# Moving the split activations to the other end of SBUF

## The chip, the cores and the metric

The kernel runs on one core of a Trainium2 chip. The metric is the device time of one execution in microseconds; smaller is better. The time before is the median of three runs. The time of the one execution that was profiled stands in the table below, since all rows come from it.

## The reference, cut to what matters

Two transformer blocks, one after the other, on 256 tokens of width 1024, all in float32. The first block projects its normed input (`w_in`), runs two attentions with eight heads each, gates and merges them, and ends in an MLP of width 4096. The second block projects again (`w_in_2`), mixes by spatial gating and a dilated attention, and ends in PEER, which is most of the time:

```
q = (xb @ w_query).reshape(PEER_TOKEN_BLOCK, PEER_HEADS, 2, D_KEY // 2)
...
g = jax.nn.softmax(sc, axis=-1)
u = expert_u[e]
act = jax.nn.gelu(jnp.einsum('td,thkd->thk', xb, u).astype(jnp.float32))
return jnp.einsum('thk,thkd->td', (g * act).astype(xb.dtype), expert_v[e])
```

Here 16 experts of 16,384 are chosen for each of the 256 tokens and 8 heads. The kernel doesn't gather them: it computes `x @ expert_u.T` for all experts, multiplies by a dense table of weights, and multiplies the result by `expert_v`. Both tables have 64 MB.

## The kernel before, in words

**Split products.** Each float32 operand of a large product is split in two parts, a rounded one and the rest: `wh` and `wl` for weights, `hh` and `hl` for activations. `mm3` (L164) makes one product of three matmuls: high by high, high by low, low by high, with `hh` and `wh` the high parts. TensorE takes two operands from SBUF: the weights that it loads (the stationary operand) and the ones that it streams through.

**Two kinds of stage.** In a *station* stage (`stations`, L288: w_gate, w_up, w_query, expert_u) the stored weights are stationary and the activations are streamed, 256 columns a matmul (two blocks of 128 tokens). A unit has two tiles of 1024 columns, 24 matmuls each, so 48 matmuls. In the other stages (`projecting` L251, `rows_product` L272, `down` L613, `v_units` L1042) the activations are stationary and the stored weights are streamed, mostly 512 columns a matmul.

**Weights.** `weights` (L107) takes tiles in turn from a cycle of pools. SP's queue loads `raw` (512 KB each), ACT copies it to `wh` (L115), and VectorE or GpSimd subtracts to give `wl` (L121). The pool `ring` has four buffers each of `raw`, `wh` and `wl`. From w_branch to w_query the cycle alternates `wkx, ring` (L564), and for the MLP two places of the right-hand pool `wk` are added behind those eight (L600). In the expert stages there is only `ring`.

**Activations.** `parts` (L210) allocates `hh` and `hl`, 8192 bytes of each partition for either. Where it is called without a pool they come from `hp`, which has one buffer of each and is used for the first projections and w_gate (L422), w_out (L568), w_in_2 (L628), and the PEER input that w_query and expert_u use (L721); at the end two tiles of it hold the residual (L1062). The MLP's own `hh` and `hl` (L591) come from the right-hand pool `wk`, and w_branch streams `oah`, `oal`, `obh`, `obl` from a right-hand pool too.

**SBUF.** A pool lies on the left or the right and is a stack: a later pool lies further in, and one that is closed gives its bytes back. Bytes per partition, as the kernel before has them:

| tiles | pool, side | from | to |
|---|---|---|---|
| raw, four buffers | ring, left | 19,744 | 36,128 |
| wh, four buffers | ring, left | 36,128 | 52,512 |
| wl, four buffers | ring, left | 52,512 | 68,896 |
| small things | small, left | 68,896 | 70,176 |
| hh, hl | hp, left | 70,176 | 86,560 |
| further left pools from here on | xp, wk1, wkx, pk, ab, pv | 86,560 | |
| wh, four buffers from w_branch to w_query | wkx, left | 123,008 | 139,392 |
| ah, two buffers in expert_v | pv, left | 152,096 | 156,192 |
| hh, hl of the MLP | wkm (`wk`), right | 161,760 | 178,144 |
| oah, the first of w_branch's four | wk1b, right | 192,480 | 196,576 |
| wh, two buffers in the MLP | wkm (`wk`), right | 206,816 | 215,008 |
| right end of the pools | | | 229,344 |

**Order of the work in PEER.** w_query has four station units and expert_u 64. TensorE's instructions are kept in program order (`in_line`, L137). During the first 32 units of expert_u (L982) VectorE also does the selection of experts (`route`). During the last 32 (L1032) each step of 12 matmuls is followed by the products that make the dense table of weights (`weighted`, L992): for two tokens VectorE makes two one-hot tiles each, `m1` and `m2` (L1019, L1020, six buffers each), and TensorE multiplies those of two earlier tokens; VectorE then multiplies the results into `acts` (L1008, L1011). After that expert_v runs with 64 units of 24 matmuls, with `ah` and `al` stationary.

Of the kernel before, what the change touches and what calls it, by code (L numbers as in the profile page):

```python
# [75 lines left out]
def block_kernel(ctx: ExitStack, tc: tile.TileContext, a, out, dbg=None):  # L76
# [3 lines left out]
    const = ctx.enter_context(tc.tile_pool(name="const", bufs=1))  # L80
    ring = ctx.enter_context(tc.tile_pool(name="ring", bufs=1))
    small = ctx.enter_context(tc.tile_pool(name="small", bufs=4))
    hp = ctx.enter_context(tc.tile_pool(name="hp", bufs=1))
    ps = ctx.enter_context(tc.tile_pool(name="ps", bufs=1, space=PSUM))
    dram = ctx.enter_context(tc.tile_pool(name="dram", bufs=1, space=DRAM))
    xres = dram.tile([P, TB, D], F32, name="xres")
# [1079 lines left out]
```

## Time and profile before

| | |
|---|---|
| median of 3 runs | 1369.34 us (1367.41 to 1370.09) |
| profiled execution | 1366.17 us |
| its span, first to last instruction | 1364.4 us |
| PE busy | 1320.8 us, 97% |
| PEld (weight loads, beside PE) busy | 1178.1 us, 86% |
| DVE (VectorE) busy | 982.0 us, 72% |
| ACT busy | 667.1 us, 49% |
| POOL (GpSimd) busy | 198.0 us, 15% |
| mean granted TensorE clock | 0.993 |

PE is TensorE. The busy time of an engine is the union of its instructions' durations. Matmuls are pipelined: a matmul's row lasts about 0.28 us for 256 columns while the next one starts some 0.12 us after it, so a busy TensorE says little, and the distance of starts says more. The chain of waits is followed back from the last instruction, at each step to what released it or to the instruction before it on its engine. A row of windows has the window, its length, then the busy time of PE, PEld, DVE, ACT and POOL, each with its count of instructions, and then the granted clock, the DMA share and GB/s.

### The profile page before, as it was taken

What the parts mean: (1) busy time and instruction counts of PE and PEld (TensorE: products, weight loads), DVE (VectorE), ACT (ScalarE), POOL (GpSimd) and SP (SyncE); (2) the same over time, 40 slices, a digit from 0 to 9 for tenths busy, and PEclk for the clock granted to TensorE, in tenths of its full rate; (3) what the DMA queues carried; (4) which work ended last, traced back from release to release, by engine and by line L of the source; (5) the groups of instructions that cost most, each with busy time, mean ns of one, the idle gap of its engine ahead of it and who ended that gap; (6) DMA issues with size and microseconds to landing.
All of it is one profiled execution on the core that took longest, in us unless ns stands there. A gap on an engine that the chain in (4) does not pass through costs nothing.

```text
span 1364.4 us, 22115 instructions
## 1 busy us (share of the span) xinstructions
PE 1320.8 (97%) x8324; PEld 1178.1 (86%) x8324; DVE 982.0 (72%) x2255; ACT 667.1 (49%) x1018; POOL 198.0 (15%) x103
## 2 busy tenths in 40 slices
PE   6999898999998999999999999999999999999997
PEld 5788896799986677999999999999978888888886
DVE  6666678555568795799994799999975555555555
ACT  5576545444444655355454444443435444544443
POOL 2221224322235336200000000000000000000001
PEclk9999999999999999999999999999999999999999
DMA  7453464666645425356666544444456666666662
GB/s 282 159 182 113 145 214 142 209 188 187 191 136 187 127 76 190 103 177 191 177 190 181 166 140 140 140 140 140 138 182 192 197 189 197 192 194 189 197 194 86
DMA packets 64187, 230.61 MB, mean 169 GB/s; under 512 B 7280, under 2 KB 7696, under 8 KB 63952
## 3 DMA queue, kind: packets, MB, share of 16 engines
q1 hardware_dynamic: 61632, 221.03, 52.5%
q0 software_dynamic: 1728, 6.07, 1.2%
q10 hardware_dynamic: 720, 2.10, 0.4%
q8 instruction: 65, 1.06, 0.3%
q14 instruction: 42, 0.34, 0.1%
HBM read 227.07 MB, written 2.10 MB: 168 GB/s over the span
## 4 chain that ended last, share of the span: by engine, by line
PE 90%; DVE 6%; ACT 2%; DMA 1%; issue 1%; SPq 0%; ACTq 0%; DVEq 0%
PE acc L135 52%; PE mid L135 35%; DVE wl L121 2%; PE tps L145 2%; DMA x<-in_x_dram 1%; ACT wh L115 1%; PE tps L135 1%; DVE x L244 0%; DVE ny L234 0%; DVE at_s L340 0%; ACT ny L206 0%; DVE rope_t L311 0%; DMA raw<-in_w_branch_dram 0%; DVE hl L174 0%; DVE at_s L332 0%
## 5 line engine op out<-in xcount | busy, mean ns | idle before, releaser
L115 ACT ACTIVATE wh<-raw 128x1024 fp32r<-128x1024 f32 (+2 forms) x422 | 439.2, 1047 | 421.7 <-PE mid L135 238.4
L121 DVE TENSOR_TENSOR wl<-raw,wh 128x1024 fp32r<-128x1024 f32 (+1 forms) x350 | 447.7, 1281 | 216.0 <-ACT wh L115 215.4
L135 PE MATMUL mid<-hh,wh 128*128 128x256 f32 x1280 | 372.1, 291 | 0.0
L135 PE MATMUL mid<-hh,wl 128*128 128x256 f32 x1280 | 361.2, 282 | 0.0
L135 PE MATMUL mid<-hl,wh 128*128 128x256 f32 x1280 | 361.0, 282 | 0.0
L135 PEld LDWEIGHTS mid<-hl,wh 128*128 128x128 f32 x1280 | 244.5, 191 | 0.4
L135 PEld LDWEIGHTS mid<-hh,wh 128*128 128x128 f32 x1280 | 244.1, 191 | 0.4
L135 PEld LDWEIGHTS mid<-hh,wl 128*128 128x128 f32 x1280 | 243.9, 191 | 0.0
L121 POOL TENSOR_TENSOR wl<-raw,wh 128x1024 fp32r<-128x1024 f32 (+3 forms) x72 | 176.3, 2458 | 340.4 <-ACT wh L115 297.3
L135 PE MATMUL acc<-wh,ah 128*128 128x512 f32 x512 | 200.0, 391 | 2.9 <-ACT ah L173 2.9
L135 PE MATMUL acc<-wl,ah 128*128 128x512 f32 x512 | 199.9, 390 | 0.0
L135 PE MATMUL acc<-wh,al 128*128 128x512 f32 x512 | 199.8, 390 | 0.0
L135 PE MATMUL acc<-wh,hh 128*128 128x512 f32 (+2 forms) x288 | 116.1, 403 | 1.1 <-ACT hh L173 0.9
L135 PEld LDWEIGHTS acc<-wh,ah 128*128 128x128 f32 x512 | 96.4, 188 | 23.2 <-ACT ah L173 3.1
L135 PEld LDWEIGHTS acc<-wh,al 128*128 128x128 f32 x512 | 96.6, 189 | 20.6 <-DVE al L174 0.4
L135 PEld LDWEIGHTS acc<-wl,ah 128*128 128x128 f32 x512 | 96.6, 189 | 19.9
L135 PE MATMUL acc<-wl,hh 128*128 128x512 f32 (+2 forms) x288 | 113.0, 392 | 0.6 <-POOL wl L121 0.3
L135 PE MATMUL acc<-wh,hl 128*128 128x512 f32 (+2 forms) x288 | 112.6, 391 | 0.4 <-DVE hl L174 0.2
L1020 DVE TENSOR_SCALAR m<-tok,key,gwt 128x128 f32<-128x128 f32 x256 | 89.2, 349 | 0.0
L173 ACT ACTIVATE ah<-acts 128x512 fp32r<-128x512 f32 x64 | 40.3, 632 | 91.8 <-PE acc L135 89.2
L174 DVE TENSOR_TENSOR al<-acts,ah 128x512 fp32r<-128x512 f32 x64 | 44.3, 693 | 52.8 <-ACT ah L173 52.8
L1019 DVE TENSOR_SCALAR m<-tok,key 128x128 f32<-128x128 f32 x256 | 73.7, 289 | 6.5 <-PE acc L135 5.6
(259 smaller groups left out, 1703.2 us busy)
## 6 DMA issues: line engine op xcount, KB each, us to landing
raw<-in_expert_u_dram SPq DMA_DIRECT2D x128, 512.0 KB, 3.7
raw<-in_expert_v_dram SPq DMA_DIRECT2D x128, 512.0 KB, 4.5
raw<-in_w_down_dram SPq DMA_DIRECT2D x32, 512.0 KB, 4.4
raw<-in_w_up_dram SPq DMA_DIRECT2D x24, 512.0 KB, 4.7
raw<-in_w_in_dram SPq DMA_DIRECT2D x20, 512.0 KB, 4.7
raw<-in_w_gate_dram SPq DMA_DIRECT2D x16, 512.0 KB, 4.0
raw<-in_w_out_dram SPq DMA_DIRECT2D x16, 512.0 KB, 4.7
raw<-in_w_in_n_dram SPq DMA_DIRECT2D x12, 512.0 KB, 4.6
```

Of the source, the lines that this page charges most:

```text
L115: i = act.activation(h[:, :n], raw[:, :n], AF.Copy)
L121: last_split[0] = eng.tensor_tensor(l[:, :n], raw[:, :n], h[:, :n].bitcast(F32), op=OP.subtract)
L135: in_line(pe.matmul(p, x, y, start=start, stop=stop))
L145: in_line(pe.transpose(out, src, ident))
L173: turned_[0] = act.activation(h, p, AF.Copy)
L174: vec.tensor_tensor(l, p, h.bitcast(F32), op=OP.subtract)
L1019: vec.tensor_scalar(m2, i128, key2[:, t:t + 1], None, op0=OP.is_equal)
L1020: vec.tensor_scalar(m1, i128, key1[:, t:t + 1], gwt[:, t:t + 1], op0=OP.is_equal, op1=OP.mult)
```

## The change

The pool `hp` is opened on the right side. It stays the first pool that is opened there, and it is open until the end.

```
-    hp = ctx.enter_context(tc.tile_pool(name="hp", bufs=1))
+    hp = ctx.enter_context(tc.tile_pool(name="hp", bufs=1, side="right"))
```

## Rows read from the trace of the kernel before

**Rows 1.** Page, chain that ended last, by line: shares of the span.

```profile
PE acc L135 52%; PE mid L135 35%; DVE wl L121 2%; PE tps L145 2%; DMA x<-in_x_dram 1%; ACT wh L115 1%; PE tps L135 1%; DVE x L244 0%; DVE ny L234 0%; DVE at_s L340 0%; ACT ny L206 0%; DVE rope_t L311 0%; DMA raw<-in_w_branch_dram 0%; DVE hl L174 0%; DVE at_s L332 0%
```

**Rows 2.** Chain of waits in order of time: start us, duration us, what, count.

```profile
302.60 5.57 PE acc L135 x24
308.17 5.76 PE mid L135 x48
...
540.48 5.58 PE acc L135 x24
...
581.77 97.91 PE mid L135 x816
...
1005.16 347.64 PE acc L135 x1524
```

**Rows 3.** TensorE's timeline, w_up: start us, duration us, instruction.

```profile
285.69 0.28 PE L135 MATMUL mid<-hh,wh 128*128 128x256 f32 x1
...
288.56 0.28 PE L135 MATMUL mid<-hh,wh 128*128 128x256 f32 x1
...
291.28 0.40 PE L135 MATMUL acc<-wh,mfh 128*128 128x512 f32 x1
```

**Rows 4.** TensorE's timeline, w_branch (12 matmuls) and w_up (24), weights from ring.

```profile
179.20 0.28 PE L135 MATMUL acc<-oah,wh 128*128 128x256 f32 x1
...
180.61 0.28 PE L135 MATMUL acc<-obh,wh 128*128 128x256 f32 x1
...
266.15 0.28 PE L135 MATMUL mid<-hh,wh 128*128 128x256 f32 x1
...
268.98 0.39 PE L135 MATMUL acc<-wh,mfh 128*128 128x512 f32 x1
```

**Rows 5.** Windows in expert_u: busy us of each engine, with counts.

```profile
600.00:650.00 50.00, 50.00 (x419) 50.00 (x418) 50.00 (x134) 25.20 (x30) 0.00 (x0) 1.00 0.63 191
...
740.00:780.00 40.00, 40.00 (x339) 40.00 (x338) 23.64 (x53) 18.71 (x27) 0.00 (x0) 1.00 0.58 170
780.00:820.00 40.00, 40.00 (x343) 40.00 (x342) 37.58 (x121) 17.72 (x32) 0.00 (x0) 1.00 0.45 137
820.00:860.00 40.00, 40.00 (x343) 40.00 (x342) 38.53 (x121) 18.40 (x33) 0.00 (x0) 1.00 0.48 145
860.00:900.00 40.00, 40.00 (x342) 40.00 (x341) 39.08 (x126) 17.29 (x32) 0.00 (x0) 1.00 0.47 139
900.00:940.00 40.00, 40.00 (x343) 40.00 (x342) 39.66 (x121) 14.90 (x30) 0.00 (x0) 1.00 0.44 139
940.00:980.00 40.00, 40.00 (x343) 40.00 (x342) 40.00 (x124) 16.64 (x34) 0.00 (x0) 1.00 0.46 138
```

**Rows 6.** Timeline of ACT, VectorE and TensorE: one tile of expert_u's first half.

```profile
636.40 1.06 ACT L115 ACTIVATE wh<-raw 128x1024 fp32r<-128x1024 f32 x1 [1.34 <-PE mid L135]
...
639.50 1.23 DVE L121 TENSOR_TENSOR wl<-raw,wh 128x1024 fp32r<-128x1024 f32 x1
...
644.96 0.28 PE L135 MATMUL mid<-hh,wh 128*128 128x256 f32 x1
```

**Rows 7.** Chain of waits, last steps of expert_u.

```profile
996.97 1.43 PE mid L135 x12
...
998.85 1.43 PE mid L135 x12
1000.28 0.91 PE acc L135 x8
1001.19 0.29 DVE m L1019
```

**Rows 8.** Chain of waits, first attention with w_gate, and its end.

```profile
90.41 3.07 PE acc L135 x24
...
119.05 2.88 PE acc L135 x24
...
155.13 3.71 DMA raw<-in_w_branch_dram
```

## The prediction

> **What bounds the kernel now.** I read the chain of waits first, by line and then in order of time. By line it is TensorE's matmuls nearly everywhere [rows 1], so a change that TensorE does not feel is worth nothing, and one that it feels must be followed to the next engine. In order of time the chain shows long runs of matmuls without a gap: 816 in 97.91 us in the first half of expert_u, 1524 in 347.64 us in expert_v [rows 2]. A row's own duration is of no use here, because matmuls overlap; what counts is the pitch, from one start to the next. It is 97.91 / 816 = 120.0 ns for a matmul of 256 columns in expert_u. Then I read TensorE's timeline for the same matmul in other stages, and here the change has its place: the pitch is not the same everywhere. In w_up, which streams its own hh and hl from the right-hand pool, 24 matmuls with weights from the ring take 291.28 - 288.56 = 2.72 us, 113.3 each; the 24 before them, with weights from wkx, 288.56 - 285.69 = 2.87 us, 119.6 each [rows 3]. With weights from the right-hand pool (the last two places of the cycle) 48 take 5.76 us, 120.0 each [rows 2]. Shape, operands, PSUM tile and loop are the same in these three; only the places in SBUF differ. Two more stretches with weights from the ring give a third value: 24 in w_up take 268.98 - 266.15 = 2.83 us, 117.9 each, and 12 in w_branch, which streams oah and obh from the right, 180.61 - 179.20 = 1.41 us, 117.5 each [rows 4]. I looked at all ring tiles: of ten in w_up nine settle at 113.3 (two of them after a few slower ones) and one at 117.9; of eight in w_branch all go at 117.8. Within a tile the pitch keeps its value.
>
> **Where the change puts things.** No instruction, loop or DMA is added, removed or moved, so no queue is passed by anything. hp holds 8192 + 8192 bytes of each partition for the whole kernel, opened before every pool that follows and never closed. It goes from 70,176 to the right end, 229,344 - 16,384 = 212,960. const, ring and small lie before it and stay; every other pool, left or right, moves down by 16,384. So which tiles lie over which is the same as before, and with it every wait that comes of reused space. What differs is the distance between the tiles that move and the ring that does not. The rows can be ordered in two ways. By ends: streamed tile and weights at one end, 120.0 (expert_u, w_up's right-hand tiles); at opposite ends, 113.3 or 117.8. By the remainder of their distance in units of 128 bytes (it is the same for all tiles of a pair of pools, since buffers lie 4096 apart and each k steps 512 on both sides): 70,176 - 36,128 (expert_u) and 161,760 - 206,816 (w_up, right) leave 0 and go at 120.0; 161,760 - 36,128 (w_up, ring) and 192,480 - 36,128 (w_branch, ring) leave 64 and go at 113.3 or 117.8; 161,760 - 123,008 (w_up, wkx) leaves 96 and goes at 119.6. After the change 212,960 - 36,128 = 176,832 leaves 64, at opposite ends: by either order it falls among the rows with 113.3 or 117.8. No row shows this very place, so the bounds are 113.3 and 120.0, and I take 113.3 where a stream runs long, the nearer of the two lower values in loop and PSUM tile, although w_branch lies nearer to the new place.
>
> **The terms.** (1) expert_u's first 32 units, without expert products between: 32 x 48 x (120.0 - 113.3) = 10.2 us. VectorE must keep up. It is busy 50.00 of 50 us in 600 to 650 [rows 5], so there it can't go faster, and TensorE at 5.76 - 5.44 = 0.32 us less a unit eats up its lead. The lead is read from one tile: ACT writes its wh at 636.40, as soon as TensorE has left that buffer; VectorE's split, 1.23 us long, starts at 639.50 and TensorE takes the tile at 644.96, 4.2 us after the split [rows 6]. Some 12 units to here cost 3.9 us, just inside it; in 740 to 780 VectorE is busy 23.64 of 40 and the lead is won back. I take 0.2 us for the pinch: 10.0. If the lead fails earlier, I lose up to 2.
>
> (2) The second 32 units, with two expert products' worth of VectorE work behind every 12 matmuls. A step, 1.43 us of 12 matmuls of 256 columns and then the products, is 998.85 - 996.97 = 1.88 us [rows 7]; TensorE would get it down by 12 x 6.67 = 0.08 us, about 10 us over 125 steps. But VectorE has almost none to give: idle 2.42, 1.47, 0.92, 0.34 and 0.00 us in the 40 us stretches from 780 to 980 [rows 5], and after TensorE's last matmul here, 1000.28 + 0.91, VectorE still works alone from 1001.19 until expert_v starts at 1005.16 [rows 2, 7]. With TensorE at 1.80 of 1.88 a stretch of 40 us would take 38.3; VectorE needs 37.58 in the first, leaving 0.74 us of idle, and is the bound from the second on. So what goes is 2.42 + 1.47 + 0.92 + 0.34 - 0.74 = 4.4 us, and what is late next is VectorE: TensorE waits for the one-hot tiles, and its own gain of 10 shrinks to 4.4. Bounds 3 and 5.2.
>
> (3) w_gate, streamed from hp into the first attention: 24 matmuls take 3.07 us early and 2.88 later [rows 8], 128 and 120 each, broken up by other work. At 113.3, 384 matmuls would give 2.5 us; broken streams need not settle at the low value, and the stage ends on other things, last the landing of w_branch's first weights, 3.71 us [rows 8], whose buffer comes free earlier if TensorE is earlier. I take half, 1.2. (4) w_query: half its eight tiles have ring weights, 96 x 6.7 = 0.6 us less; the wkx half goes from remainder 32 to 96, whose row has 119.6, so at best nothing: I take 0.4 together.
>
> (5) The projections, with hp's tiles as weights and the ring streamed, 512 columns: 24 take 5.58 us now, 232.5 each; in w_down, whose weights lie at the right, 24 take 5.57 [rows 2]. So nothing, with 1.5 us either way. (6) expert_v: ah and al go down with the other left pools; ah at 152,096 - 36,128 leaves remainder 0 before and, 16,384 lower, after. I take its 347.64 / 1524 = 228.1 ns as it is.
>
> Sum: 10.0 + 4.4 + 1.2 + 0.4 = 16.0 us off the profiled execution's 1366.17 (span 1364.4), so 1350.2. The median of the runs is 1369.34, 3.2 us above that execution; what I predict is compared with such a median, so 1369.34 - 16.0 = 1353.3.
>
> A rule of the Trainium skill speaks against all this. SBUF — State Buffer, section "Who interferes with whom", gives TensorE two independent read ports, one for the streamed operand and one for the weight load, and says "PE and ACT never wait on anyone". By it the place of hp could not matter and the sum would be 0, which is rival (b). The trace disagrees: 113.3, 117.9 and 120.0 ns in one stage with only places differing [rows 2 to 4].
>
> **The rivals.** (a) The stream settles at 117.8, as in w_branch. Then term 1 is 1536 x 2.2 = 3.4 us, term 2 is what VectorE allows at 39.4 us for 40: 0.6 + 0.6 + 0.6 + 0.3 = 2.0 (its idle of 2.42, 1.47 and 0.92 each less by 0.6), terms 3 and 4 together 0.6: 6.0 us, 1363.3. For it: all of w_branch, and the one tile in w_up. Against it: nine tiles of ten in the stage that is most like expert_u.
>
> (b) The pitch stays at 120.0 in expert_u, because what the rows in w_up show comes of something else there, such as its alternation with w_down: no change, 1369.3. Against it: the right-hand tiles in the same alternation go at 120.0.
>
> (c) Slower: the order by remainder is wrong, expert_u stays at 120, and expert_v pays, since ah and al come 16,384 bytes nearer to the ring. The price is from w_down's mixed pitch, 5.57 / 24 = 232.1 against 228.1, 1536 x 4.0 = 6.1 us: 1375.4. It decides as soon as expert_v's pitch rises by more than expert_u's falls, matmul for matmul at about 1 to 1. Against it: ah, like hp now, keeps its remainder.
>
> **How the numbers follow.** My forecast has 0.55, (a) 0.25, (b) 0.13, (c) 0.07. About 0.2% of the time, 2.7 us, is what can be told from no change. The forecast and (a) are both faster by more: 0.80; (b) is the same, 0.13; (c) slower, 0.07. The forecast's own range goes from 1349 (w_gate whole, VectorE's idle all gone, projections 1.5 better) to 1358 (term 2 at 3, term 1 less by 2, projections 1.5 worse). With (a) and what its terms can miss the range is 1348.5 to 1366, leaving out (b) and (c).
>
> **What would show it.** In the changed profile: 24 ring matmuls of expert_u's first half 2.72 us apart, the run that is 97.91 us long for 816 now at 113.3 each; the second half's steps at 1.80 us at first and then stretched by waits for the one-hot tiles, with VectorE at 40.00 of 40 from early on; expert_v at 228 and the projections at 232 as before. A pitch of 117.8 is rival (a), 120.0 is (b). I am wrong in term 2 if the step reaches 1.80 us to the end, and in the whole if the pitch in expert_u falls but the stage doesn't get shorter.

## The result and the profile after

The changed kernel takes 1357.02 us (median of 4 runs, 1355.48 to 1358.35), the kernel before 1368.38 (4 runs of the same batch): ratio 0.9916, 95% interval 0.9897 to 0.9935. It is faster by 11.4 us where 16.0 were forecast; its median lies 3.7 us above the 1353.3 that was predicted, and inside the range of 1348.5 to 1366. A second batch of the unaltered changed kernel (below) gave 1353.69 against 1369.2, faster by 15.5. The profiled execution is one of 1355.48 us, its span 1353.7 (before: 1366.17 and 1364.4).

The chain by line, from the page after, answers to [rows 1]: TensorE still holds most of it, VectorE's split at L121 a little more than before.

```profile
PE acc L135 52%; PE mid L135 29%; DVE wl L121 3%; PE tps L145 2%; DMA x<-in_x_dram 1%; ACT wh L115 1%; DVE eq L896 1%; DVE ef L898 1%; PE tps L135 1%; DVE at_s L340 1%; DVE eq L893 1%; DVE x L244 0%; ACT ny L206 0%; DVE rope_t L311 0%; DVE ny L234 0%
```

The chain in order of time, after (start us, duration us, what, count), answers to [rows 2, 7, 8]:

```profile
90.89 2.94 PE acc L135 x24
...
118.95 2.75 PE acc L135 x24
...
303.56 5.57 PE acc L135 x24
309.12 5.76 PE mid L135 x48
...
542.68 5.58 PE acc L135 x24
...
583.35 40.83 PE mid L135 x360
...
687.93 54.46 PE mid L135 x478
...
984.91 1.38 PE mid L135 x12
986.29 0.44 PE acc L135 x4
986.73 1.42 PE mid L135 x12
...
994.54 347.55 PE acc L135 x1524
```

In expert_u 360 matmuls take 40.83 us, 113.4 ns each, and 478 take 54.46, 113.9; 816 took 120.0 each in [rows 2]. w_down (5.57), w_up's right-hand tiles (5.76), the projections (5.58) and expert_v (347.55) stand where they stood. In the second half of expert_u 12 matmuls take 1.38 and 1.42 us by turns, where [rows 7] have 1.43.

Windows in expert_u, after (busy us of PE, PEld, DVE, ACT, POOL with counts, granted clock, DMA share, GB/s), answer to [rows 5]:

```profile
600.00:650.00 50.00, 50.00 (x444) 50.00 (x443) 50.00 (x146) 27.03 (x32) 0.00 (x0) 1.00 0.61 189
650.00:700.00 50.00, 49.37 (x436) 49.17 (x435) 49.86 (x122) 26.58 (x34) 0.00 (x0) 1.00 0.63 194
740.00:780.00 40.00, 40.00 (x352) 40.00 (x351) 28.62 (x75) 19.33 (x30) 0.00 (x0) 1.00 0.56 171
780.00:820.00 40.00, 40.00 (x349) 40.00 (x348) 38.47 (x125) 18.74 (x33) 0.00 (x0) 1.00 0.48 141
820.00:860.00 40.00, 40.00 (x350) 40.00 (x349) 39.23 (x126) 17.98 (x33) 0.00 (x0) 1.00 0.47 142
...
940.00:980.00 40.00, 40.00 (x349) 40.00 (x349) 40.00 (x124) 15.91 (x32) 0.00 (x0) 1.00 0.46 135
```

TensorE gets 444 matmuls into 600 to 650 us where it had 419, and 349 or 350 into each stretch from 780 on that is shown, where it had 342 or 343.

Where the time went, by stage (us from the stage's first matmul to the next stage's, read from TensorE's timeline; w_up ends with its last matmul, and the rest of w_down counts with the way to w_query; expert_v goes to its last matmul; "again" is the second profile of the changed kernel, from the experiments):

| stage | before | after | again |
|---|---|---|---|
| start to w_gate | 87.56 | 88.06 | 87.53 |
| w_gate, first attention | 74.43 | 73.17 | 73.59 |
| w_branch to w_up | 101.30 | 103.02 | 100.84 |
| w_up, with w_down between | 117.38 | 117.38 | 117.38 |
| rest of w_down, to w_query | 166.48 | 167.73 | 166.47 |
| w_query | 27.74 | 27.41 | 27.41 |
| expert_u, first half | 185.91 | 176.72 | 176.68 |
| expert_u, second half | 239.20 | 234.40 | 234.39 |
| gap ahead of expert_v | 5.16 | 6.68 | 6.63 |
| expert_v | 349.95 | 349.87 | 350.13 |

The stages with a term lose 1.26 + 0.33 + 9.19 + 4.80 - 1.52 = 14.1 us. Three stages that the change does not touch take 0.50 + 1.72 + 1.25 = 3.5 us longer in the first profile of the changed kernel, and not in the second.

### The profile page after: what moved, and what is told of

It reads as the page before. It is cut to its first block, busy times and chain, and to the rows that moved or that the text cites. A ratio compares the mean times of both kernels' runs of the same rounds, so it can differ in the third digit from the quotient of the medians.

```text
span 1353.7 us, 22115 instructions
## 1 busy us (share of the span) xinstructions
PE 1308.4 (97%) x8324; PEld 1165.2 (86%) x8324; DVE 979.7 (72%) x2255; ACT 666.4 (49%) x1018; POOL 197.4 (15%) x103
## 4 chain that ended last, share of the span: by engine, by line
PE 84%; DVE 10%; issue 2%; ACT 2%; DMA 1%; SPq 0%; POOL 0%; ACTq 0%; DVEq 0%
PE acc L135 52%; PE mid L135 29%; DVE wl L121 3%; PE tps L145 2%; DMA x<-in_x_dram 1%; ACT wh L115 1%; DVE eq L896 1%; DVE ef L898 1%; PE tps L135 1%; DVE at_s L340 1%; DVE eq L893 1%; DVE x L244 0%; ACT ny L206 0%; DVE rope_t L311 0%; DVE ny L234 0%
## 5 line engine op out<-in xcount | busy, mean ns | idle before, releaser
L121 DVE TENSOR_TENSOR wl<-raw,wh 128x1024 fp32r<-128x1024 f32 (+1 forms) x350 | 449.2, 1286 | 208.9 <-ACT wh L115 208.5
L135 PE MATMUL mid<-hh,wh 128*128 128x256 f32 x1280 | 367.2, 287 | 0.0
L135 PE MATMUL mid<-hh,wl 128*128 128x256 f32 x1280 | 355.8, 278 | 0.6 <-DVE wl L121 0.6
L135 PE MATMUL mid<-hl,wh 128*128 128x256 f32 x1280 | 355.9, 278 | 0.0
L135 PEld LDWEIGHTS mid<-hl,wh 128*128 128x128 f32 x1280 | 241.9, 189 | 0.4
L135 PEld LDWEIGHTS mid<-hh,wh 128*128 128x128 f32 x1280 | 241.0, 188 | 0.4
L135 PEld LDWEIGHTS mid<-hh,wl 128*128 128x128 f32 x1280 | 240.5, 188 | 0.8 <-DVE wl L121 0.8
L121 POOL TENSOR_TENSOR wl<-raw,wh 128x1024 fp32r<-128x1024 f32 (+3 forms) x72 | 175.0, 2441 | 343.9 <-ACT wh L115 301.1
L135 PE MATMUL acc<-wh,ah 128*128 128x512 f32 x512 | 200.0, 391 | 2.9 <-ACT ah L173 2.9
L135 PE MATMUL acc<-wl,ah 128*128 128x512 f32 x512 | 199.9, 390 | 0.0
L135 PE MATMUL acc<-wh,al 128*128 128x512 f32 x512 | 199.8, 390 | 0.0
L135 PE MATMUL acc<-wh,hh 128*128 128x512 f32 (+2 forms) x288 | 117.4, 408 | 1.5 <-ACT hh L173 1.5
L135 PEld LDWEIGHTS acc<-wh,ah 128*128 128x128 f32 x512 | 96.6, 189 | 23.2 <-ACT ah L173 3.1
L135 PE MATMUL acc<-wh,hl 128*128 128x512 f32 (+2 forms) x288 | 114.1, 396 | 1.0 <-DVE hl L174 0.8
L135 PE MATMUL acc<-wl,hh 128*128 128x512 f32 (+2 forms) x288 | 114.2, 396 | 0.6 <-POOL wl L121 0.3
L135 PEld LDWEIGHTS acc<-wh,al 128*128 128x128 f32 x512 | 96.5, 188 | 20.4 <-DVE al L174 0.2
L135 PEld LDWEIGHTS acc<-wl,ah 128*128 128x128 f32 x512 | 96.5, 189 | 19.9
L1020 DVE TENSOR_SCALAR m<-tok,key,gwt 128x128 f32<-128x128 f32 x256 | 94.5, 371 | 0.0
L1019 DVE TENSOR_SCALAR m<-tok,key 128x128 f32<-128x128 f32 x256 | 79.2, 310 | 3.8 <-PE acc L135 3.0
```

Of the source, the lines that this page charges most:

```text
L121: last_split[0] = eng.tensor_tensor(l[:, :n], raw[:, :n], h[:, :n].bitcast(F32), op=OP.subtract)
L135: in_line(pe.matmul(p, x, y, start=start, stop=stop))
L1019: vec.tensor_scalar(m2, i128, key2[:, t:t + 1], None, op0=OP.is_equal)
L1020: vec.tensor_scalar(m1, i128, key1[:, t:t + 1], gwt[:, t:t + 1], op0=OP.is_equal, op1=OP.mult)
```

## The experiments

Two theories at the start. Theory 1: the pitch follows the remainder of a distance, streamed tile less weights. Theory 2: it follows the ends of SBUF, or what hp lies beside. In the experiments up to left192 and right256, padding pools shift hp by less than 256 bytes, and some other pools with it, as said at each; no instruction changes. Four lines of padding move the line numbers, so L139 there is L135. A chain row is start us, duration us, what, count.

**left64**: hp stays left, 64 bytes further on.

```diff
+    pad0 = ctx.enter_context(tc.tile_pool(name="pad0", bufs=1))
+    pad0.tile([P, 16], F32, name="pad0")
     hp = ctx.enter_context(tc.tile_pool(name="hp", bufs=1))
+    pad1 = ctx.enter_context(tc.tile_pool(name="pad1", bufs=1))
+    pad1.tile([P, 16], F32, name="pad1")
```

> hp stays on the left; 64 unused bytes of a partition lie ahead of it and 64 behind it, so its distance to the ring is 64 modulo 128 and no other pair of pools changes its remainder. Theory 1 (the remainder of the distance decides): expert_u's first half goes at 113.3 ns a matmul as in the changed kernel, and the time is the changed kernel's, 1357 us, within 2. Theory 2 (the ends decide: both at one end is slow): 120.0 ns and the time of the kernel before, 1368.

Measured: 1370.76 us, ratio 1.0022 (1.0012 to 1.0032). Its chain:

```profile
582.95 96.11 PE mid L139 x816
...
1001.33 355.84 PE acc L139 x1524
```

The pitch in expert_u is 96.11 / 816 = 117.8 ns, neither theory's value, and expert_v went from 228.1 to 233.5, 8.3 us in its stage. The 128 bytes of padding had moved ah and al by 128, which modulo 128 is nothing: so the order by 128 falls, and the two sizes fit a modulus of 256, where hp's remainder is now 64 and ah's 128.

**right0**: hp stays right, 64 bytes further in, and the other pools on the right 128.

```diff
+    pad0 = ctx.enter_context(tc.tile_pool(name="pad0", bufs=1, side="right"))
+    pad0.tile([P, 16], F32, name="pad0")
     hp = ctx.enter_context(tc.tile_pool(name="hp", bufs=1, side="right"))
+    pad1 = ctx.enter_context(tc.tile_pool(name="pad1", bufs=1, side="right"))
+    pad1.tile([P, 16], F32, name="pad1")
```

> hp lies on the right as in the changed kernel, but 64 unused bytes before its outer end bring its distance to the ring to 0 modulo 128. Theory 1 (remainder): 120.0 ns a matmul in expert_u's first half and about 1368 us, the gain gone. Theory 2 (ends): 113.3 ns and 1357 us.

Measured: 1366.05 us, ratio 0.9983 (0.9973 to 0.9993); its chain:

```profile
583.57 96.83 PE mid L139 x816
...
1003.84 348.14 PE acc L139 x1524
```

118.7 ns: most of the gain is gone with hp at the right end. The end alone does not give 113.3.

**align64** and **align0** ask whether the start of hp, rather than a distance, counts. Both push the left pools on by 32 bytes and hp and the other pools on the right inward by 96 (align64) or 32 (align0), so the distance leaves 64 or 128 modulo 256 with other starts than in the two kernels above.

```diff
+    padc = ctx.enter_context(tc.tile_pool(name="padc", bufs=1))
+    padc.tile([P, 8], F32, name="padc")
     const = ctx.enter_context(tc.tile_pool(name="const", bufs=1))
...
+    pad0 = ctx.enter_context(tc.tile_pool(name="pad0", bufs=1, side="right"))
+    pad0.tile([P, 24], F32, name="pad0")
     hp = ctx.enter_context(tc.tile_pool(name="hp", bufs=1, side="right"))
```

(pad0 is 8 wide in align0.)

> The changed kernel with 32 unused bytes ahead of all left pools and 96 at the right end: ring and hp both start at a multiple of 64 bytes (before at 32 past one), their distance stays 64 modulo 128. Theory 1 (only the remainder decides): 113.3 ns in expert_u's first half, 1357 us. Theory 3 (a start 32 past a multiple of 64 costs part of the pitch as well): less than 113.3 in expert_u, down to 107, and less than 227 in expert_v; 1340 to 1350 us.

> As the kernel with both ring and hp at multiples of 64 bytes, but with 32 unused bytes at the right end, so that their distance is 0 modulo 128. Theory 1 (only the remainder): 120.0 ns in expert_u's first half, 1368 us. Theory 3 (start at multiples of 64 matters too): less than 120, and expert_v below 227; 1345 to 1360 us.

Measured: align64 1363.67 us, ratio 0.9958 (0.9944 to 0.9972); align0 1367.08, ratio 0.9985 (0.9976 to 0.9995). The chain of align64, then of align0:

```profile
584.78 96.11 PE mid L139 x816
...
1003.15 347.40 PE acc L139 x1524
```

```profile
585.17 96.83 PE mid L139 x816
...
1005.47 348.44 PE acc L139 x1524
```

align64 repeats left64's 96.11 us (remainder 64) and align0 right0's 96.83 (128), with other starts and, for remainder 64, at the other end. So in expert_u it is the distance modulo 256, not the start (theory 3 is out) nor the end.

**left192** and **right256** test the mended theory from both sides: hp at the left with the remainder of the changed kernel, and hp at the right with that of the kernel before. Everything else keeps its place modulo 256.

```diff
+    pad0 = ctx.enter_context(tc.tile_pool(name="pad0", bufs=1))
+    pad0.tile([P, 48], F32, name="pad0")
     hp = ctx.enter_context(tc.tile_pool(name="hp", bufs=1))
+    pad1 = ctx.enter_context(tc.tile_pool(name="pad1", bufs=1))
+    pad1.tile([P, 16], F32, name="pad1")
```

right256 has the same two pads on the right side around the changed kernel's hp.

> hp on the left as before the change, with 192 unused bytes of a partition ahead of it and 64 behind it: its distance to the ring leaves 192 modulo 256, as in the changed kernel, and all other pairs of pools keep their remainder modulo 256. Theory 1, mended (the remainder modulo 256 of the distance between streamed tile and weights decides): 113.4 ns a matmul in expert_u's first half, 226.7 in expert_v, and the changed kernel's time, 1357 us within 2, with hp still beside the ring. Theory 2 (the end of SBUF decides): 118 to 120 ns and 1363 to 1369 us.

> hp at the right end as in the changed kernel, with 192 unused bytes outside it and 64 inside it: its distance to the ring leaves 0 modulo 256 as in the kernel before, all other pairs keep the changed kernel's remainder. Theory 1, mended (remainder modulo 256): 120.0 ns a matmul in expert_u's first half and the time of the kernel before, 1368.8 us within 1.5. Theory 2 (ends): 113 to 118 ns, 1357 to 1363 us.

Measured: left192 1355.68 us, ratio 0.9904 (0.9888 to 0.9921); right256 1368.93, ratio 1.0006 (0.9993 to 1.0018). The chain of left192, then of right256:

```profile
582.74 81.63 PE mid L139 x720
...
994.46 347.52 PE acc L139 x1524
```

```profile
585.35 97.91 PE mid L139 x816
...
1008.76 348.66 PE acc L139 x1524
```

The whole gain without the move (81.63 / 720 = 113.4 ns), and the move without the gain (97.91 / 816 = 120.0). Theory 2 is out. The distances of the kernel before and right256, 34,048 and 176,640 bytes, differ by 557 x 256, and so do those of left192 and the changed kernel; so a modulus of 512 would not put them together.

**before_light** and **after_light** leave out two of VectorE's multiplications by the expert products (L970 and L1011) from the kernel before and the changed one, so that VectorE is idle for 3.3 us or more in each 40 us of expert_u's second half. If VectorE bounds that half, it must get shorter.

```diff
             if k:
                 g = acts[1][:, :k, ts]
-                vec.tensor_tensor(g, g, pv[:, P // 2:P // 2 + k, :], op=OP.mult)
...
-            vec.tensor_tensor(g[:, :, :t0], p[:, :, :t0], g[:, :, :t0], op=OP.mult)
```

> The kernel before, leaving out two multiplications by the table of weights on VectorE (L970 and L1011), so that part of the experts goes unweighted; TensorE's work is the same. If TensorE sets the second half of expert_u before the change, its steps stay at 1.88 us (239 us for the half) and only the 5.2 us to expert_v shrink, to about 3: 1366 us. If VectorE already sets part of it, the half itself gets shorter, 236 us or less.

> The changed kernel, leaving out the same two multiplications. Theory V (VectorE is what keeps the second half of expert_u at 234.4 us where TensorE could do 229): with the load gone the half falls to 229 to 230 us, the 6.7 us to expert_v to 3, total 1348 to 1350. Theory P (TensorE itself sets it, because after each interruption by the table's products the stream settles at 113.4 or at 117.8 ns, 116.2 on the mean): the half stays at 233 to 235 us, only the 6.7 us fall to 3, total 1353.

Measured: before_light 1366.85 us, ratio 0.9981 (0.997 to 0.9993); after_light 1352.21, ratio 0.9882 (0.9864 to 0.99). The second half takes 239.20 and 234.39 us, as without the edit; the gap ahead of expert_v is 3.56 us in both. The chain of before_light:

```profile
870.05 1.43 PE mid L135 x12
871.49 0.45 PE acc L135 x4
871.93 1.43 PE mid L135 x12
```

The chain and a window of after_light:

```profile
870.20 1.38 PE mid L135 x12
871.58 0.44 PE acc L135 x4
872.03 1.42 PE mid L135 x12
873.44 0.45 PE acc L135 x4
```

```profile
780.00:820.00 40.00, 40.00 (x349) 40.00 (x349) 36.49 (x111) 18.06 (x34) 0.00 (x0) 1.00 0.46 145
```

With 3.51 us of idle on VectorE in this window the step is still 1.38 or 1.42 us and then 0.44 or 0.45. So TensorE itself sets the half, and its 12 matmuls go at 115 to 118 ns between two interruptions, not at 113.3. VectorE costs the gap at the end, 6.68 against 3.56 us, and no more of this half.

**after_again, wkx192, wkx192_pool** ask how far one execution speaks for the kernel, and look for a version that beats both. wkx192 puts the second weight pool at remainder 192 as well; wkx192_pool also gives GpSimd one split in eight during expert_u.

```diff
+    padx = b1.enter_context(tc.tile_pool(name="padx", bufs=1))
+    padx.tile([P, 40], F32, name="padx")
     wkx = b1.enter_context(tc.tile_pool(name="wkx", bufs=1, reuse_waits="tile"))
...
-    helpers[0] = [vec]
+    helpers[0] = [vec] * 7 + [pool]
...
+    helpers[0] = [vec]
     pv = late_pools.enter_context(tc.tile_pool(name="pv", bufs=1, reuse_waits="tile"))
```

(The lines on helpers are in wkx192_pool alone.)

> The changed kernel once more, unaltered, beside the two that follow. Expected: median 1355 to 1358 us, ratio to the kernel before 0.990 to 0.993. If the two spells at half clock of 6.83 us in the profile of the changed kernel belong to the placement (theory T), they stand again at the same places and the time is 1355.5 or more; if they belong to the single execution (theory U), their lengths or places differ here, and with spells of 3.41 us the time falls to some 1352 to 1355 us.

> The changed kernel with the second weight pool (wkx, used from w_branch to w_query) moved up by 160 bytes, so that the distance from its tiles to the streamed ones has the remainder 192 modulo 256 instead of 96. Theory M (the pitch at 256 columns follows that remainder in every stage): the matmuls that load from this pool in w_up (240 in the rows), w_branch (72) and w_query (92) go from 119.5 to about 113.5 ns, 404 x 6.0 ns = 2.4 us less; where its tiles are themselves streamed at 512 columns (w_down and the projections, about 410 matmuls at 233.9 ns on average) the remainder becomes that of the ring's tiles (64, 230.3 ns), some 1.4 us less; together 3.8 us, so 3.5 to 4 us under the changed kernel of this batch. Theory N (the pitch falls, but in these stages TensorE waits for the splits of ScalarE and VectorE, so little of it reaches the end): under 1.5 us. Theory O (the remainder rules only while one pool is in use, not where two alternate): pitch stays 119.5 and the time the same within 1 us.

> As the kernel before this one in the batch, and in expert_u one low-part subtraction in eight is done by GpSimd instead of VectorE (in expert_v VectorE does all, as before). Theory P (VectorE costs only the pinch in the first half, 0.6 us, and the longer gap ahead of expert_v, 6.68 against 3.56 us): the gap shrinks to 3.6 to 5 us, the time is 1.5 to 3.5 us less than the kernel before this one. Theory Q (GpSimd's subtraction, 2.4 us against VectorE's 1.2, slows VectorE's tensor_tensor beside it or makes its unit late): TensorE waits for wl at L121 with GpSimd as the releaser, and the time is the same or up to 5 us more.

Measured, beside 1369.2 us for the kernel before: after_again 1353.69 (1352.11 to 1355.01), ratio 0.9892 (0.9878 to 0.9907), below the median that was expected and within the times of theory U; wkx192 1354.75 (1352.63 to 1358.64), 0.9904 (0.9888 to 0.992); wkx192_pool 1358.65 (1355.64 to 1361.92), 0.9921 (0.9905 to 0.9938). Neither can be told from the changed kernel as a gain; no version here beats it.

The windows at one place (columns as above; the figure before the DMA share is the granted clock) of the kernel before, the changed kernel, and after_again:

```profile
424.00:428.00 4.00, 4.00 (x19) 3.25 (x18) 1.11 (x1) 2.93 (x3) 2.41 (x1) 1.00 0.00 0
```

```profile
424.00:428.00 4.00, 4.00 (x10) 3.14 (x11) 0.52 (x1) 1.06 (x1) 0.72 (x1) 0.50 0.00 0
```

```profile
424.00:428.00 4.00, 4.00 (x21) 3.29 (x20) 2.42 (x3) 3.00 (x4) 3.36 (x2) 1.00 0.14 16
```

With the granted clock at 0.50, the lower level of 1.2 GHz, TensorE gets 10 matmuls through instead of 19 or 21; ahead of it, in 418 to 422 us, it had been busy 1.79 of 4 us. Spells like this stand in all three profiles, at about the same work (near 162, 228 and 421 us) and of different lengths, and two profiles of one kernel differ in them (theory U): the stage that this spell lies in takes 167.73 us in one and 166.47 in the other. The 3.5 us of the three untouched stages came with the execution, not with the change.

In w_up TensorE's timeline shows the pad of wkx192 at work: 24 matmuls with weights from wkx, first in the changed kernel, then in wkx192.

```profile
264.24 0.28 PE L135 MATMUL mid<-hh,wh 128*128 128x256 f32 x1
...
267.11 0.28 PE L135 MATMUL mid<-hh,wh 128*128 128x256 f32 x1
```

```profile
262.99 0.28 PE L135 MATMUL mid<-hh,wh 128*128 128x256 f32 x1
...
265.72 0.28 PE L135 MATMUL mid<-hh,wh 128*128 128x256 f32 x1
```

2.87 us became 2.73, and over all its matmuls the pool's mean (gaps of 0.15 us or more left out) went from 119.6 to 113.3 ns in w_branch, 119.7 to 114.7 in w_query and 119.5 to 115.7 in w_up: theory M of the pitch. But only 0.9 us of w_up's 117.38 and 0.5 of w_query's 27.41 went; the stages between were no shorter, and in this execution the stream of expert_u's first half sat at 117.8 for eleven tiles on end, from 644 to 675 us (94.20 us for 816, 115.4 each). The forecast of 3.8 us is a miss; whether 1 us is left of it can't be told.

In wkx192_pool theory P is wrong too: the gap is 7.20 us, the second half 235.85. The windows there show why little was won:

```profile
600.00:650.00 50.00, 48.93 (x432) 48.74 (x431) 49.93 (x135) 25.67 (x30) 9.31 (x2) 1.00 0.60 181
...
780.00:820.00 40.00, 40.00 (x350) 40.00 (x349) 39.43 (x128) 18.81 (x33) 2.38 (x1) 1.00 0.48 145
```

VectorE is busier in 780 to 820 (39.43 us) than in the changed kernel (38.47), although it has fewer splits. Two of GpSimd's splits fill 9.31 us in the first window; one of them took 6.92 us, where the median is 2.40, and VectorE's longest split in expert_u was 2.46 us against 1.23 in wkx192. TensorE never waits for a split of GpSimd there, so theory Q's sign is not seen either. Of the 6.7 us by which this profile is longer than that of wkx192, 3.6 lie between w_branch and w_up, which the edit on helpers does not touch; the granted clock is 0.50 there from 248 to 252 us, and 1.00 in wkx192.

## Why the prediction was right, and where not

The main step held: hp's place changes the pitch of the matmuls that stream it, and in expert_u it falls from 120.0 to 113.4 ns.

*Term 1*, 10.0 predicted, 9.2 measured. The pinch came, later and dearer than I took it. The chain of the changed kernel at that place, and its waits of TensorE (us in total, times, longest):

```profile
685.01 1.73 DVE eq L893
686.75 1.15 DVE wl L121
687.89 0.04 issue
```

```profile
PE mid L135 <- DVE wl L121: 0.6, 1, 0.6
```

VectorE's lead is used up at the twentieth unit or so, and TensorE waits 0.6 us for one split, against 0.2 in the sum. The wait is TensorE's idle; by the distance of starts it costs more:

```profile
687.03 0.28 PE L135 MATMUL mid<-hl,wh 128*128 128x256 f32 x1
687.93 0.39 PE L135 MATMUL mid<-hh,wl 128*128 128x256 f32 x1 [0.63 <-DVE wl L121]
688.16 0.28 PE L135 MATMUL mid<-hh,wh 128*128 128x256 f32 x1
```

These two steps take 1.13 us instead of 2 x 0.113, so the pinch costs 0.9. Of the 10.2 us without a pinch that leaves 9.3; the last 0.1 is a pitch of 113.36 ns on the mean instead of 113.3.

*Term 2*, 4.4 predicted, 4.8 - 1.5 = 3.3 measured, and its cause was wrong. The step that failed is "So what goes is 2.42 + 1.47 + 0.92 + 0.34 - 0.74 = 4.4 us, and what is late next is VectorE". Part of its idle is indeed gone (1.53, 0.77 and 0.00 us left in the windows above, for 2.42, 1.47 and 0.00), but TensorE never waits for it there, and taking work off VectorE moves nothing: before_light and after_light. What limits the gain is the pitch between interruptions, 12 matmuls in 1.40 us on average where I had 12 x 113.3 = 1.36. So about half of TensorE's 10 us was never to be had, for another reason than mine, and that 4.8 lies near 4.4 is luck. VectorE's share comes afterwards, in the gap.

*Terms 3 and 4*, 1.2 and 0.4: 1.26 (0.84 in the second profile) and 0.33. In w_gate 24 matmuls take 2.94 and later 2.75 us where [rows 8] have 3.07 and 2.88; 0.13 us in each of 16 would be 2.1, and the half of it that reaches the stage's end is what I took for broken streams.

*Terms 5 and 6*, nothing: the projections at 5.58 us and expert_v at 347.55 [rows 2].

Of the two orders, that by ends fell with left192 and right256, and that by 128 with left64's expert_v and with right0 and align0, which it would have at 120.0. That both had named the right rows for this one move is luck: 176,832 leaves 64 modulo 128 and 192 modulo 256, and the rows in w_up and w_branch have the same 192. Rival (a)'s 117.8 is what remainder 64 gives in expert_u, and a value at which remainder 192 sits at times (w_branch's ring tiles, [rows 4]; wkx192's first half). The rows ahead of the change could not tell which of the two values expert_u would take; that it took 113.4 was the likelier of two guesses, not something that they showed. Rival (b) is out: nothing but 256 bytes of padding, 192 of them ahead of hp, takes 13 us off in left192. This speaks against the rule of the Trainium skill (SBUF — State Buffer, "Who interferes with whom") that TensorE's two read ports are independent, by which the place of hp could not matter; what makes the place count inside the chip, no run shows. Rival (c) did not come, but left64 shows that its mechanism exists: expert_v does pay when ah's distance changes, 8.3 us in its stage at remainder 128 instead of 0 (I had priced it at 6.1).

Of the 3.7 us by which the first median lies above the forecast, 1.9 are the terms (14.1 for 16.0); the rest is within what executions of this kernel differ by, 1352.11 to 1358.35 in the eight of the two batches.

## What to carry to other kernels

Read the pitch of one and the same matmul in several stages; if it differs, compare the SBUF addresses of its two operands early. A pad of some bytes between two pools is a cheap experiment, and it must be tested for what else it moves. A bound read from an engine's idle is an argument; leaving out part of that engine's work shows in one run whether it holds.

## What the runs showed of the hardware

In expert_u the pitch of a float32 matmul with a weight load of its own follows the distance in bytes, streamed operand less weights, modulo 256. With 256 columns the long runs of its first half give:

| remainder | ns | kernels |
|---|---|---|
| 0 | 120.0 | before, right256 |
| 64 | 117.8 | left64, align64 |
| 128 | 118.7 | right0, align0 |
| 192 | 113.4 (115.4 in one profile) | changed kernel twice, left192, wkx192 |

In w_up wkx's tiles, at 96, have 119.6. With 512 columns, in expert_v, remainder 0 has 228.1 (347.55 us for 1524) and 128 has 233.5, so the order of these two is the other way round.

The table is no rule for every stage. At 192 the stream has two values, 113.3 and 117.8, and may stay at the higher one for some tiles before it falls. At 64 it has the same two: in w_query of align64 three of the four ring tiles go at 113.3, here 21 matmuls in 2.38 us.

```profile
560.67 0.28 PE L139 MATMUL mid<-hh,wh 128*128 128x256 f32 x1
...
563.05 0.28 PE L139 MATMUL mid<-hh,wh 128*128 128x256 f32 x1
```

Which value it takes is not settled by the place alone. In w_branch the ring tiles of the kernel before go at 117.8 ([rows 4]: 12 in 1.41 us), and in before_light, which is the same program up to there, at 113.4 once the first of them is past (12 in 1.36 us):

```profile
178.80 0.28 PE L135 MATMUL acc<-oah,wh 128*128 128x256 f32 x1
...
180.16 0.28 PE L135 MATMUL acc<-obh,wh 128*128 128x256 f32 x1
```

In expert_u two kernels at 64 stay at 117.8, and those at 192 spend most of their tiles at 113.3; the times of each placement repeat from run to run (left192 1355.36 to 1355.92, align64 1361.0 to 1363.95), so there it is the place and not the execution. What makes the stream choose was not tried, nor why 256.
